# Where the activation operands begin in SBUF, relative to the weights, in a two-network fp32 kernel

## The chip, the cores and the metric

The kernel runs on one core of one Trainium2 chip, as one program. The time is device microseconds for one execution, from three timed runs; beside them stands one further execution that was profiled, and all rows come from that one. Busy times, waits and spacings are read from that profile.

## What is computed

Two small transformers run one behind the other on a sequence of 256 positions of width 1024, all in float32. The first has two layers (differential attention, then neighbourhood attention, each followed by a SwiGLU block of width 2816 and a gated side input); the second has a mixer of a convolution and pooling, then an attention mixer, each followed by a convolutional gated block of width 2816. Cut to what matters here:

```
for i in range(2):                                   # first network
    h = h + (diff_attention, neighborhood_attention)[i](rmsnorm(h, norm_mix[i]))
    hn = rmsnorm(h, norm_ffn[i])
    h = h + (silu(hn @ w_gate[i]) * (hn @ w_up[i])) @ w_down[i]
    h = h + sigmoid(rmsnorm(h, norm_ple[i]) @ ple_w_gate[i]) * (p[i] @ ple_w_proj[i])
x = rmsnorm(h, norm_final)
for layer in range(2):                               # second network
    h = h + (even_mixer, odd_mixer)[layer](rmsnorm(h, mix_norm_g_2[layer]))
    u, g = split(rmsnorm(h, ffn_norm_g_2[layer]) @ w_in_2[layer])
    h = h + (silu(causal_dwconv(u) + conv_b) * g) @ w_out_2[layer]
return rmsnorm(h, final_norm_g_2)
```

Nearly all arithmetic is in the products with weight matrices of 1024 rows or columns.

## The kernel before

Every product with weights is made three times, on the high and low parts of both operands. `Weights.split` (lines 74 to 98) takes a staged float32 chunk of 128 x 1024, writes the rounded part `w_hi` on ScalarE (line 88) and the remainder `w_lo` on VectorE (line 89). Activations are split in the same way into `u_hi` and `u_lo` (`split_act`, lines 225 to 228, written at lines 260 and 262, or at the ends of the attention and mixer stages), and the middle of each feed-forward block into the two halves of a tile `m` (line 735, written at lines 727 and 728). `mm3` then issues three matmuls of 256 columns with 128 x 128 weights, all through line 199: `u_hi,w_hi`, `u_lo,w_hi` and `u_hi,w_lo`. In the rows a matmul is named `out<-moving,stationary`: `ps_g<-u_hi,w_hi` streams `u_hi` past weights `w_hi`. In the value products of the attention stages the roles are exchanged (`ps_v<-w_hi,u_hi`).

A feed-forward block (`ffn`, lines 730 to 748) has 22 steps. Each makes a pair of outputs from `u` (48 matmuls into `ps_g`) and computes a middle `m`; every second step two middles are multiplied with the down matrix into four accumulators (`acc`, 24 matmuls for each middle). So TensorE's work there goes in pieces of 96 matmuls with `u` and 48 with `m`. The middles take their slots in turn from the tags `qh` and `kh`, of two slots each, which in the attention stages hold the high parts of the queries and keys.

No table sets an order here: a tile framework gives out slots from pools, in the order in which pools and tags are first used, and puts a wait where a slot is used again. Together the pools take some 223 KB of each partition, so that room is short. The weight slots are 4,096 bytes each and all begin at 224 bytes past a multiple of 256. A tile `gap` of 64 bytes (lines 114 to 116) stands behind them, so that every slot of the pools `acts` and `work` begins at 32 past a multiple of 256: 64 bytes further than the weights, modulo 256. This remainder is called the distance below. Since all steps inside a tile are multiples of 512 bytes, the distance holds for every matmul of `u` and `m` with weights.

Of the kernel before, what the change touches and what calls it, by code (L numbers as in the profile page):

```python
# [10 lines left out]
F32 = mybir.dt.float32  # L11
F32R = mybir.dt.float32r
# [6 lines left out]
S = 256  # L19
KT = D // 128  # L20
# [86 lines left out]
def network(ctx: ExitStack, tc: tile.TileContext, x_t, p_t, cols, b_v, na_bias, t5_bias, w_mats, out):  # L107
    nc = tc.nc
# [1 line left out]
    const = ctx.enter_context(tc.tile_pool(name="const", bufs=1))  # L110
    stage = ctx.enter_context(tc.tile_pool(name="stage", bufs=N_STAGE))
    split = ctx.enter_context(tc.tile_pool(name="split", bufs=N_HI))

    shift = ctx.enter_context(tc.tile_pool(name="shift", bufs=1))
    gap = shift.tile([128, 16], F32, name="gap")
    nc.gpsimd.memset(gap, 0.0)
    acts = ctx.enter_context(tc.tile_pool(name="acts", bufs=2))
    work = ctx.enter_context(tc.tile_pool(name="work", bufs=2))
    small = ctx.enter_context(tc.tile_pool(name="small", bufs=2))
    psum = ctx.enter_context(tc.tile_pool(name="psum", bufs=1, space=PSUM))  # L120
# [45 lines left out]
    h = const.tile([128, KT, S], F32, name="h")  # L166
# [55 lines left out]
            due.remove(d)  # L222
            d[2]()

    def split_act(tag="u"):
        hi = acts.tile([128, KT, S], F32R, tag=tag + "h", name="u_hi")
        lo = acts.tile([128, KT, S], F32R, tag=tag + "l", name="u_lo")
        return hi, lo

# [188 lines left out]
    def qkv_group(n, g, kind, bv, steps):  # L420
        q = work.tile([128, 2, S], F32, tag="q", bufs=1, name="q")
        k = work.tile([128, 2, S], F32, tag="k", bufs=1, name="k")

        def parts(x, tag):
            hi = work.tile([128, 2, S], F32R, tag=tag + "h", name=tag + "_hi")
            lo = work.tile([128, 2, S], F32R, tag=tag + "l", name=tag + "_lo")
            nc.scalar.activation(hi, x, AF.Copy)
            nc.vector.tensor_sub(lo, x, hi.bitcast(F32))
            return x, hi, lo

        v = work.tile([128, 2, S], F32, tag="v", name="v")
        u = n.u
        ps = pair(u)
        if kind == "na":
            t = work.tile([128, 2, S], F32, tag="qb", bufs=1, name="qb")
            nc.vector.tensor_mul(t, ps, bc2(n.R))
            for i in range(2):
                nc.scalar.activation(q[:, i, :], t[:, i, :], AF.Identity, bias=b_q8[:, 2 * g + i:2 * g + i + 1],
                                     scale=0.125)
        else:  # L440
            nc.vector.scalar_tensor_tensor(q, ps, 0.125, bc2(n.R), op0=OP.mult, op1=OP.mult)
        q = parts(q, "q")
        ps = pair(u)
        if kind == "na":
            t = work.tile([128, 2, S], F32, tag="qb", bufs=1, name="kb")
            nc.vector.tensor_mul(t, ps, bc2(n.R))
            for i in range(2):
                nc.scalar.activation(k[:, i, :], t[:, i, :], AF.Identity, bias=col("b_k", 2 * g + i), scale=1.0)
        else:
            nc.vector.tensor_mul(k, ps, bc2(n.R))  # L450
        k = parts(k, "k")
        steps(q, k, v)
        if kind == "od" and g == 0:
            z = small.tile([128, 2, 8], F32, tag="zf", bufs=1, name="zf")
            pz = [psum.tile([128, 264], F32, tag=f"acc{2 + t}", name="pz") for t in range(2)]
            kk = 0
            for n_k in (3, 3, 2):
                hi, lo = W.take(n_k * 264)
                for i in range(n_k):
                    for t in range(2):  # L460
                        for a, b in ((0, hi), (1, hi), (0, lo)):
                            mm(pz[t], u[a][:, kk, t * 128:(t + 1) * 128], b[:, i * 264:(i + 1) * 264],
                               kk == 0 and (a, b) == (0, hi), kk == 7 and b is lo)
                    kk += 1
                    if kk % 2 == 0:
                        tick()
            for t in range(2):
                nc.scalar.activation(v[:, t, :], pz[t][:, :256], AF.Copy, scale=n.rstd[:, t:t + 1])
                nc.vector.scalar_tensor_tensor(z[:, t, :], pz[t][:, 256:264], n.rstd[:, t:t + 1],
                                               ct[:, COL["b_f"]:COL["b_f"] + 8], op0=OP.mult, op1=OP.add)  # L470
            fox_prepare(z, extra)
            return
        pv = psum.tile([128, 2, S], F32, tag="acc3", name="ps_v")
        for half in range(2):
            hi, lo = W.take(1024)
            for i in range(4):
                kk = 4 * half + i
                for t in range(2):
                    for c, (a, b) in enumerate(((0, hi), (1, hi), (0, lo))):
                        mm(pv[:, t, :], u[a][:, kk, t * 128:(t + 1) * 128], b[:, i * 256:(i + 1) * 256],  # L480
                           kk == 0 and t == 0 and c == 0, kk == 7 and c == 2, skip_group_check=True)
                if i % 2 == 1:
                    tick()
        for t in range(2):
            if kind == "na":
                nc.vector.scalar_tensor_tensor(v[:, t, :], pv[:, t, :], n.rstd[:, t:t + 1], bv,
                                               op0=OP.mult, op1=OP.add)
            else:
                nc.scalar.activation(v[:, t, :], pv[:, t, :], AF.Copy, scale=n.rstd[:, t:t + 1])
# [14 lines left out]
    def small_constants():  # L504

        nc.vector.scalar_tensor_tensor(dist, dist, -1.0, dist, op0=OP.mult, op1=OP.max)
        for hd in range(8):
            nc.vector.tensor_scalar(da_tiles[hd // 4][:, hd % 4], dist, -2.0 ** (-8.0 * (hd + 1) / 8), None, op0=OP.mult)
        nc.vector.tensor_scalar(tri, off[:, :128], 0.0, None, op0=OP.is_ge)
        for g, w in enumerate(POOL_WINDOWS):  # L510
            nc.vector.tensor_scalar(rcnt[:, g, :], rcnt[:, g, :], float(w), None, op0=OP.min)
        nc.vector.reciprocal(rcnt, rcnt)
        nc.vector.tensor_scalar(causal, off, 128.0, NEG, op0=OP.is_gt, op1=OP.mult)
        l = COL["lam"]
        pr = work.tile([128, 2, 64], F32, tag="dump", bufs=1, name="pr")
        for i in range(2):
            nc.vector.tensor_mul(pr[:, i, :], ct[:, l + 128 * i:l + 128 * i + 64], ct[:, l + 128 * i + 64:l + 128 * i + 128])
        nc.vector.tensor_reduce(lam[:, 0:2], pr, AX.X, OP.add)
        nc.scalar.activation(lam[:, 0:2], lam[:, 0:2], AF.Exp)
        lam_init = 0.8 - 0.6 * math.exp(-0.3 * 0)  # L520
        nc.vector.scalar_tensor_tensor(lam[:, 2:3], lam[:, 1:2], -lam_init, lam[:, 0:1],
                                       op0=OP.add, op1=OP.subtract)
        nc.vector.tensor_scalar(sg, col("subln", 0), 1.0 - lam_init, None, op0=OP.mult)
        nc.vector.tensor_scalar(b_q8, ct[:, COL["b_q"]:COL["b_q"] + 8], 0.125, None, op0=OP.mult)
        nc.vector.tensor_mul(g_fm, ct[:, COL["norm_final"]:COL["norm_final"] + 8], ct[:, COL["mix2"]:COL["mix2"] + 8])


    def da_steps(g, q, k, v, bias, o, emitted):
        for p in range(2):
# [23 lines left out]
            def values(p=p, box=box):  # L553
# [4 lines left out]
                        mm(po[:, qt * 128:(qt + 1) * 128], at[:, kk * 256 + qt * 128:kk * 256 + (qt + 1) * 128],  # L558
                           v[:, kk, p * 128:(p + 1) * 128], kk == 0, kk == 1)
                st = small.tile([128, 8], F32, tag="st", bufs=4, name="st2")  # L560
                dump = work.tile([128, 128], F32, tag="dump", bufs=1, name="dump")
                for qt in range(2):
                    nc.scalar.activation(dump, po[:, qt * 128:(qt + 1) * 128], AF.Square, accum_out=st[:, qt:qt + 1])
                nc.vector.tensor_scalar(st[:, 2:4], st[:, 0:2], 1.0 / 128, 1e-5, op0=OP.mult, op1=OP.add)
# [165 lines left out]
    def ffn(n, middle, gain_next, finish=None):  # L730
        acc = Acc(FT)
        mids = {}
        for j in range(FT):
            ps = pair(n.u)
            m = work.tile([128, 2, S], F32R, tag=("qh", "kh")[j % 2], name="m")
            mids[j] = (m[:, 0, :], m[:, 1, :])
            middle(j, ps, n.R, mids[j])
            if j >= 2 and j % 2 == 0 and j < FT - 2:
                acc.step(mids.pop(j - 2), j - 2)
                acc.step(mids.pop(j - 1), j - 1)  # L740
        for j in range(FT - 4, FT - N_LAST):
            acc.step(mids.pop(j), j)
        if finish is None:
            nn, done = next_norm(gain_next)
        else:
            nn, done = finish()
        acc.last([mids.pop(j) for j in range(FT - N_LAST, FT)], FT - N_LAST, done)
        return nn
# [97 lines left out]
    def pool_out(ps, i0):  # L846
        for i in range(2):
            g = i0 + i
# [12 lines left out]
            nc.vector.tensor_mul(av[:, :16], cur[:, 16:32], rcnt[:, g, :])  # L861
            nc.vector.tensor_scalar(av[:, 16:], cur[:, 32:], 1.0 / w, None, op0=OP.mult)
            nc.vector.tensor_sub(av, av, uu[:, 16:])
            m = work.tile([128, 2, S], F32R, tag=("qh", "kh")[g % 2], name="pool_m")
            ph, pl = m[:, 0, :], m[:, 1, :]
            nc.scalar.activation(ph, av, AF.Copy)
            nc.vector.tensor_sub(pl, av, ph.bitcast(F32))
# [89 lines left out]
    rstd_a(n)  # L957
    for i in range(2):
        for t in range(2):
            o = work.tile([128, 512], F32, tag=("qh", "kh")[t], name="o")  # L960
            if t:
                nc.vector.tensor_scalar(o, po[i][t], n.rstd[:, t:t + 1], None, op0=OP.mult)
            else:
# [138 lines left out]
```

## Time and profile before

| | |
|---|---|
| three timed runs | 1276.21, 1270.15, 1274.69 us; median 1274.69 us |
| profiled execution | 1266.52 us, of which 1264.8 us from the first to the last instruction |
| granted TensorE clock, mean | 0.997 of full speed |
| TensorE matmul, weight load | busy 1242.2 us, 1211.8 us |
| VectorE, ScalarE, GpSimd | busy 932.7 us, 697.5 us, 31.6 us |
| read from HBM | 219.74 MB, 175 GB/s over the span |

A matmul's recorded duration (about 280 ns) overlaps those of its neighbours, which start 113 to 118 ns apart, so durations do not add up. What a matmul costs in a stream is the spacing between starts, which is read from the chain of waits (so many matmuls in so many microseconds) or from a window (its length divided by the matmuls in it, where TensorE never idles).

### The profile page before, as it was taken

Reading aid. Unit: us, or ns where it says so; the run is one execution under the profiler, and the core shown is the slowest. Engines: PE = TensorE matmul, PEld = TensorE weight load, DVE = VectorE, ACT = ScalarE, POOL = GpSimd, SP = SyncE. Lnnn points to the kernel's source line nnn. Section 1 sums busy time; section 2 is a strip of 40 time slices with the busy share of each in tenths; the row PEclk is TensorE's granted clock in tenths of the full one; section 3 lists DMA queues with packets and bytes.
Section 4 is the critical chain, followed back from the end, with each engine's and each line's share of the span. In section 5 each row is a group of like instructions: output and inputs, shape, how many; then the busy total and the mean of one; then the engine's idle time right before and its main releaser. Section 6 shows DMA issues by size and latency. Waiting matters only on the chain.

```text
span 1264.8 us, 25714 instructions
## 1 busy us (share of the span) xinstructions
PE 1242.2 (98%) x10448; PEld 1211.8 (96%) x10448; DVE 932.7 (74%) x1708; ACT 697.5 (55%) x1178; POOL 31.6 (2%) x55
## 2 busy tenths in 40 slices
PE   6999999999999999999999999999999999999997
PEld 6999999999988999999999999999999899999997
DVE  7876866667876677666678888777787766877774
ACT  6776644445666654444456456455566565554543
POOL 1011000000010000000000000000000000000000
PEclk9999999999999999999999999999999999999998
DMA  8465566654656436565545475555545343655530
GB/s 291 156 198 182 172 192 201 199 182 147 223 165 177 166 122 205 187 199 186 176 146 192 141 239 190 192 185 192 192 152 186 115 133 131 204 185 189 191 120 34
DMA packets 62936, 222.46 MB, mean 176 GB/s; under 512 B 7265, under 2 KB 7777, under 8 KB 62689
## 3 DMA queue, kind: packets, MB, share of 16 engines
q1 hardware_dynamic: 60768, 214.52, 51.4%
q0 software_dynamic: 1616, 5.77, 2.0%
q8 instruction: 82, 1.34, 0.4%
q10 hardware_dynamic: 432, 0.53, 0.1%
q14 instruction: 38, 0.30, 0.1%
HBM read 219.74 MB, written 1.05 MB: 175 GB/s over the span
## 4 chain that ended last, share of the span: by engine, by line
PE 86%; DVE 5%; issue 3%; ACT 3%; DMA 1%; POOL 1%; POOLq 0%; SPq 0%; DVEq 0%; ACTq 0%
PE ps_g L199 49%; PE acc L199 24%; PE ps_v L199 5%; PE ps_S L199 3%; DVE w_lo L89 2%; PE ps_V L199 2%; PE ps_t L385 1%; ACT w_hi L88 1%; ACT u_hi L260 1%; DMA stage<-w_da_qkv 1%; POOL rstd L285 1%; DVE ssq L253 1%; ACT sq L245 0%; PE pz L199 0%; DVE h L363 0%
## 5 line engine op out<-in xcount | busy, mean ns | idle before, releaser
L88 ACT ACTIVATE w_hi<-stage 128x1024 fp32r<-128x1024 f32 (+2 forms) x413 | 428.9, 1041 | 420.6 <-PE ps_g L199 164.7
L89 DVE TENSOR_TENSOR w_lo<-stage,w_hi 128x1024 fp32r<-128x1024 f32 (+2 forms) x413 | 495.6, 1202 | 204.3 <-ACT w_hi L88 201.6
L199 PE MATMUL ps_g<-u_hi,w_hi 128*128 128x256 f32 x2048 | 575.6, 282 | 8.5 <-ACT w_hi L88 7.0
L199 PE MATMUL ps_g<-u_lo,w_hi 128*128 128x256 f32 x2048 | 571.5, 280 | 0.4 <-DVE u_lo L262 0.4
L199 PE MATMUL ps_g<-u_hi,w_lo 128*128 128x256 f32 x2048 | 570.6, 279 | 0.8 <-DVE w_lo L89 0.8
L199 PEld LDWEIGHTS ps_g<-u_hi,w_hi 128*128 128x128 f32 x2048 | 384.8, 188 | 13.0 <-ACT w_hi L88 7.0
L199 PEld LDWEIGHTS ps_g<-u_hi,w_lo 128*128 128x128 f32 x2048 | 385.4, 188 | 1.3 <-DVE w_lo L89 1.0
L199 PEld LDWEIGHTS ps_g<-u_lo,w_hi 128*128 128x128 f32 x2048 | 385.1, 188 | 1.3 <-DVE u_lo L262 0.6
L199 PE MATMUL acc<-m,w_hi 128*128 128x256 f32 x1408 | 248.5, 279 | 0.2 <-DVE m L728 0.2
L199 PEld LDWEIGHTS acc<-m,w_hi 128*128 128x128 f32 x1408 | 214.4, 188 | 1.0 <-DVE m L728 0.5
L199 PE MATMUL acc<-m,w_lo 128*128 128x256 f32 x704 | 195.6, 278 | 0.0
L199 PEld LDWEIGHTS acc<-m,w_lo 128*128 128x128 f32 x704 | 132.2, 188 | 0.0
L199 PE MATMUL acc<-u_hi,w_hi 128*128 128x256 f32 x256 | 72.7, 287 | 0.0
L199 PE MATMUL acc<-u_lo,w_hi 128*128 128x256 f32 x256 | 71.3, 280 | 0.3 <-DVE u_lo L577 0.3
L199 PE MATMUL acc<-u_hi,w_lo 128*128 128x256 f32 x256 | 71.1, 279 | 0.0
L415 ACT ACTIVATE sc<-sc,st 128x256 f32<-128x256 f32 (+1 forms) x96 | 46.1, 483 | 19.2 <-DVE st L413 19.2
L199 PE MATMUL ps_v<-w_hi,u_hi 128*128 128x256 f32 x176 | 51.1, 291 | 0.0
L199 PE MATMUL ps_v<-w_lo,u_hi 128*128 128x256 f32 x176 | 49.4, 280 | 0.0
L199 PE MATMUL ps_v<-w_hi,u_lo 128*128 128x256 f32 x176 | 49.3, 280 | 0.0
L199 PEld LDWEIGHTS acc<-u_hi,w_hi 128*128 128x128 f32 x256 | 47.8, 188 | 1.5 <-issue 0.6
L199 PEld LDWEIGHTS acc<-u_lo,w_hi 128*128 128x128 f32 x256 | 48.0, 188 | 0.5 <-DVE u_lo L577 0.5
L199 PEld LDWEIGHTS acc<-u_hi,w_lo 128*128 128x128 f32 x256 | 48.0, 188 | 0.0
(190 smaller groups left out, 1218.3 us busy)
## 6 DMA issues: line engine op xcount, KB each, us to landing
stage<-w_gu SPq DMA_DIRECT2D x88, 512.0 KB, 3.8
stage<-w_in SPq DMA_DIRECT2D x88, 512.0 KB, 3.3
stage<-w_down SPq DMA_DIRECT2D x44, 512.0 KB, 3.8
stage<-w_out SPq DMA_DIRECT2D x44, 512.0 KB, 3.3
stage<-w_na_qkv SPq DMA_DIRECT2D x24, 512.0 KB, 3.9
stage<-w_da_qkv SPq DMA_DIRECT2D x23, 512.0 KB, 4.5
stage<-w_od_in SPq DMA_DIRECT2D x22, 512.0 KB, 3.3
stage<-w_gate SPq DMA_DIRECT2D x16, 512.0 KB, 3.3
```

Source lines behind the costliest of these rows:

```text
L88: self.nc.scalar.activation(hi[:, s], t[:, s], AF.Copy)
L89: self.nc.vector.tensor_sub(lo[:, s], t[:, s], hi[:, s].bitcast(F32))
L199: nc.tensor.matmul(o, a, b, start=start, stop=stop, **kw)
L253: nc.vector.tensor_add(ssq, ssq, sq)
L260: nc.scalar.activation(n.u[0][:, 2 * b + i, :], src[:, i, :], AF.Copy, scale=gain(2 * b + i))
L285: nc.gpsimd.tensor_tensor(n.rstd, st[:, 2:4], mhalf, op=OP.pow)
L385: nc.tensor.transpose(ps[:, o:o + 128], a[:, qt, kk * 128:(kk + 1) * 128], ident)
L415: nc.scalar.activation(sc[:, i, :widths[i]], sc[:, i, :widths[i]], AF.Exp, bias=st[:, 2 + i:3 + i], accum_out=st[:, 4 + i:5 + i])
```

## The change

The tile `gap` and its memset go. `acts` has one slot for each of four tags instead of two for each of two, in the same alternation; each slot is 256 bytes longer and the operand begins 32 or 224 bytes into it. The tags `qh` and `kh` get slots that are 64 bytes longer, and the operand begins 32 (`qh`) or 16 bytes (`kh`) into them. Since all slots before them are multiples of 256 long again, the distances become: `u` 224 in the first, third, ... slot that is taken and 32 in the second, fourth, ...; middles 32 and 96 (`qh`), 144 and 208 (`kh`), in the sequence 32, 144, 96, 208 over four steps. To make room, `pr` and `dump` share the tag `fb`. All else in `work` now lies at distance 0, save the low parts of the queries, at 128; before, all of it lay at 64.

```diff
-    shift = ctx.enter_context(tc.tile_pool(name="shift", bufs=1))
-    gap = shift.tile([128, 16], F32, name="gap")
-    nc.gpsimd.memset(gap, 0.0)
-    acts = ctx.enter_context(tc.tile_pool(name="acts", bufs=2))
+    acts = ctx.enter_context(tc.tile_pool(name="acts", bufs=1))
...
-    def split_act(tag="u"):
-        hi = acts.tile([128, KT, S], F32R, tag=tag + "h", name="u_hi")
-        lo = acts.tile([128, KT, S], F32R, tag=tag + "l", name="u_lo")
-        return hi, lo
+    slot = [0]
+
+    def split_act():
+
+        i = slot[0] = slot[0] ^ 1
+        first = (8, 56)[i]
+        parts = []
+        for p, name in (("h", "u_hi"), ("l", "u_lo")):
+            t = acts.tile([128, 64 + KT * S], F32R, tag=f"u{p}{i}", name=name)
+            parts.append(t[:, first:first + KT * S].rearrange("p (k s) -> p k s", k=KT))
+        return tuple(parts)
+
+    def half_tile(tag, name):
+
+        first = {"qh": 8, "kh": 4}[tag]
+        t = work.tile([128, 16 + 2 * S], F32R, tag=tag, name=name)
+        return t[:, first:first + 2 * S].rearrange("p (a b) -> p a b", a=2)
...
-            hi = work.tile([128, 2, S], F32R, tag=tag + "h", name=tag + "_hi")
+            hi = half_tile(tag + "h", tag + "_hi")
...
-        pr = work.tile([128, 2, 64], F32, tag="dump", bufs=1, name="pr")
+        pr = work.tile([128, 2, 64], F32, tag="fb", bufs=2, name="pr")
...
-                dump = work.tile([128, 128], F32, tag="dump", bufs=1, name="dump")
+                dump = work.tile([128, 128], F32, tag="fb", bufs=2, name="dump")
...
-            m = work.tile([128, 2, S], F32R, tag=("qh", "kh")[j % 2], name="m")
+            m = half_tile(("qh", "kh")[j % 2], "m")
...
-            m = work.tile([128, 2, S], F32R, tag=("qh", "kh")[g % 2], name="pool_m")
+            m = half_tile(("qh", "kh")[g % 2], "pool_m")
...
-            o = work.tile([128, 512], F32, tag=("qh", "kh")[t], name="o")
+            o = work.tile([128, 528], F32, tag=("qh", "kh")[t], name="o")[:, :512]
```

No instruction changes its place on any engine. GpSimd has one fewer, at its start; before:

```order
L1088 UNCONDITIONAL_BRANCH [waits barrier_Pool_Activation_PE_DVE_SP_gather]
L116 MEMSET gap 128x16
L176 ISA
L176 IOTA off 128x256
```

and after:

```order
L1097 UNCONDITIONAL_BRANCH [waits barrier_Pool_Activation_PE_DVE_SP_gather]
L172 ISA
L172 IOTA off 128x256
```

The iotas stand one place earlier. On ScalarE, four of the squares into `dump` in the first attention stage name one wait fewer; one of them before:

```order
L388 ACTIVATE at<-ps_t 128x512 [waits PE_49]
L563 ACTIVATE dump,st_714<-ps_V 128x128 [waits PE_49,Activation_49]
L563 ACTIVATE dump,st_714<-ps_V 128x128 [waits Activation_49]
```

and after:

```order
L397 ACTIVATE at<-ps_t 128x512 [waits PE_49]
L572 ACTIVATE dump,st_709<-ps_V 128x128 [waits PE_49]
L572 ACTIVATE dump,st_709<-ps_V 128x128 [waits Activation_49]
```

The wait that went was one of ScalarE on its own earlier square.

## Rows read from the trace of the kernel before

**Rows 1.** The page: busy time by engine, then the chain by line.

```profile
PE 1242.2 (98%) x10448; PEld 1211.8 (96%) x10448; DVE 932.7 (74%) x1708; ACT 697.5 (55%) x1178; POOL 31.6 (2%) x55
...
PE ps_g L199 49%; PE acc L199 24%; PE ps_v L199 5%; PE ps_S L199 3%; DVE w_lo L89 2%; PE ps_V L199 2%; PE ps_t L385 1%; ACT w_hi L88 1%; ACT u_hi L260 1%; DMA stage<-w_da_qkv 1%; POOL rstd L285 1%; DVE ssq L253 1%; ACT sq L245 0%; PE pz L199 0%; DVE h L363 0%
```

**Rows 2.** What TensorE waited for: total us, times, longest.

```profile
PE ps_g L199 <- ACT w_hi L88: 7.0, 1, 7.0
PE ps_r L301 <- POOL rstd L285: 3.4, 4, 2.5
```

**Rows 3.** Chain, first feed-forward block: start us, us, what.

```profile
152.76 10.88 PE ps_g L199 x96
163.64 5.44 PE acc L199 x48
```

**Rows 4.** Chain, second feed-forward block.

```profile
490.88 11.31 PE ps_g L199 x96
502.18 5.65 PE acc L199 x48
```

**Rows 5.** Chain, third feed-forward block, where pieces of both lengths stand.

```profile
780.98 10.88 PE ps_g L199 x96
791.86 5.61 PE acc L199 x48
797.47 11.31 PE ps_g L199 x96
...
825.74 5.55 PE acc L199 x48
831.29 10.88 PE ps_g L199 x96
```

**Rows 6.** TensorE by window: bounds, length, busy (matmuls), clock, DMA share, GB/s.

```profile
139.00:313.00 174.00, 174.00 (x1538) 1.00 0.59 190
320.00:344.00 24.00, 24.00 (x206) 1.00 0.71 238
476.00:658.00 182.00, 182.00 (x1546) 1.00 0.55 182
664.00:689.00 25.00, 25.00 (x222) 1.00 0.62 208
702.00:760.00 58.00, 57.82 (x489) 1.00 0.57 186
...
1085.00:1120.00 35.00, 35.00 (x300) 1.00 0.57 191
1121.00:1140.00 19.00, 19.00 (x168) 1.00 0.59 194
1141.00:1246.00 105.00, 105.00 (x894) 1.00 0.44 146
```

**Rows 7.** Groups by line: shapes, count, busy us, mean ns, idle before.

```profile
L199 PE MATMUL ps_g<-u_lo,w_hi 128*128 128x256 f32 x2048 | 571.5, 280 | 0.4 <-DVE u_lo L262 0.4
L199 PE MATMUL acc<-m,w_hi 128*128 128x256 f32 x1408 | 248.5, 279 | 0.2 <-DVE m L728 0.2
L199 PE MATMUL acc<-m,w_lo 128*128 128x256 f32 x704 | 195.6, 278 | 0.0
L199 PE MATMUL acc<-u_hi,w_lo 128*128 128x256 f32 x256 | 71.1, 279 | 0.0
L199 PE MATMUL ps_v<-w_hi,u_lo 128*128 128x256 f32 x176 | 49.3, 280 | 0.0
...
L199 PE MATMUL ps_p<-p_part,w_hi 128*128 128x256 f32 x64 | 11.5, 278 | 0.0
```

**Rows 8.** Chain in the second attention stage.

```profile
376.63 0.44 PE ps_t L385 x4
377.07 1.37 PE ps_g L199 x12
378.44 1.41 PE ps_v L199 x12
```

**Rows 9.** By line, the memset of gap: min/median/max ns, first and last start.

```profile
L116 POOL MEMSET gap<- x1: 112/112/112, 0.7 to 0.7; 128x16 f32 x1
```

**Rows 10.** The same view of the tile dump.

```profile
L563 ACT ACTIVATE dump<-ps_V x16: 257/277/280, 46.4 to 119.5; 128x128 f32<-128x128 f32 x16
```

## The prediction

> **What bounds the kernel now.** The page comes first: TensorE is busy for 98% of the span, and the chain that ends last lies on it, with 78% in three kinds of products with weights, `ps_g`, `acc` and `ps_v` [rows 1]. Then what TensorE waits for: the longest entry is 7.0 us, once, at the start; the next totals 3.4 us [rows 2]. No feeding engine is late in the long stages, so what a change is worth there is read from the spacing of matmuls and from nothing else.
>
> The chain gives that spacing, and the reader is to see that there are two. In the first feed-forward block 96 matmuls take 10.88 us and 48 take 5.44 us, 113.3 ns each [rows 3]. In the second, the same 96 and 48 take 11.31 and 5.65 us, 117.8 ns each [rows 4]. Shapes, order and distance (64 bytes) are the same. In the third, whole pieces of either length follow one another and the rhythm changes within an `acc` piece (5.61 and 5.55 us lie between) [rows 5]. So TensorE has a fast and a slow rhythm, 0.43 us / 96 = 4.5 ns apart, and keeps either for a long time: the windows give 174.00 us / 1538 = 113.1 ns for the whole first block and 182.00 / 1546 = 117.7 ns for the whole second [rows 6]. The granted clock is 1.00 in both, so it is not the clock; and no wait marks the difference.
>
> **How much hangs on the rhythm.** The 256-column products with weights are three kinds of 2048 for `ps_g`, 1408 + 704 for `acc` from `m`, three of 256 for `acc` from `u`, three of 176 for `ps_v`: 6144 + 2112 + 768 + 528 = 9552 [rows 7]. What the slow rhythm cost in this execution, as a window's length less its matmuls at 113.3 ns [rows 6]: second block 182.0 - 175.2 = 6.8 us; 702 to 760, 57.8 - 55.4 = 2.4; 320 to 344, 0.7; fourth block 35.0 - 34.0 = 1.0 and 105.0 - 101.3 = 3.7. In the third block four pieces of 96 are slow, of which rows 5 show one, for 4 x 0.43 = 1.7, and its eight `acc` pieces are between 0.11 and 0.22 over 5.44, together 1.3. That is 17.6 us over some 6,820 matmuls. The other 2,730 lie mostly in the three attention stages, broken up by short work; there 12 matmuls take 1.41 us (117.5 ns) in one piece and 1.37 us (114.2 ns) in the piece before it [rows 8]. I take three in four as slow: 2730 x 0.75 x 4.5 ns = 9.2 us. In all the slow rhythm cost about 27 us. **Bounds:** everything fast would be 1266.5 - 27 = 1239.5 us. For everything slow, the matmuls now at 113.3 ns pay 4.5 ns more: 1538 + 222 + 168 in their windows, some 800 in the third block and 2730 x 0.25 = 680 in attention, 3,400 in all, or 15 us: 1281.5 us.
>
> The profiled execution took 1266.5 us, 8.2 us under the median of 1274.69; at 4.5 ns that is 1,800 matmuls more in the slow rhythm, well inside these bounds. The three timed runs differ by 6 us with the same program and the same addresses, so which rhythm a stage falls into is partly chance. The mean of the four executions, (1276.2 + 1270.2 + 1274.7 + 1266.5) / 4 = 1271.9 us, is the best reading of the kernel before.
>
> **The change part by part.** Nothing is moved, and no step is added. *The memset* of the gap, 112 ns on GpSimd at 0.7 us [rows 9], goes; TensorE's first wait ends on ScalarE's split of weights at 7 us [rows 2], which needs transfers and not GpSimd, so this is worth nothing; if that cover were gone it would be 0.1 us. *The tag shared by `pr`, `dump` and `fb`*: the 16 squares take 277 ns each, between 46 and 120 us [rows 10]; four lose a wait of ScalarE on itself, and `fb` itself serves the last attention stage alone. Zero; all four at a full square each would be 1.1 us. *The longer slots* change no instruction's size.
>
> *The distances* are the change. `u` goes from 64 to 224 or 32 (6,900 matmuls with `acc` from `u`), middles from 64 to 32, 144, 96, 208 (2,112), and `ps_v` from 192, seen the other way round, to 32 or 224. What a distance of 32 or 144 costs a matmul no row shows, so it is bounded by the nearest. (a) `ps_v` lies at 192 and shows 117.5 ns a matmul in one piece right behind `ps_g` at 114.2 [rows 8], and its recorded duration is 280 ns as that of `ps_g` [rows 7]: another distance, the same two rhythms. That speaks for no price at all. (b) Below: the transposes stream `ident` at distance 224 to the tile they transpose, 4 in 0.44 us, 110 ns [rows 8]. They are another kind of operation, so this is a far bound: 9552 x 3.3 ns = 32 us under the all-fast time, 1208 us. (c) Above: a third rhythm one equal step of 4.5 ns over the slow one would cost the middles 2112 x 4.5 = 9.5 us, 1291 us, and all matmuls 43 us, 1324.5 us. I take (a), the only row with the same operation at two distances. *The rest of `work`* goes to distance 0: 96 matmuls from `p_part` [rows 7] and some 240 of the scores' high and low parts; at one step each, 336 x 4.5 ns = 1.5 us either way, taken as 0.
>
> The Trainium skill speaks against the change here: in "TensorE: Matmul & The Clock Gate", Part 2, it says that TensorE reads streamed operand and weights through two independent SBUF ports, so that loading the next weights takes nothing from the running matmul. By that rule no distance can matter and the time stays; that `ps_v` at 192 keeps the known rhythms agrees, that there are two rhythms at all the page does not tell.
>
> **The rivals.** *A, forecast: the distance does not enter.* The two rhythms stay, drawn by chance; the time is that of before, 1271.9 us, with the spread of four executions, 1266 to 1277. For it: both rhythms hold for 1,500 matmuls at one and the same distance, and `ps_v`. A change of distance between `u` and `m` may be a new draw, now every 24 to 96 matmuls; were slow then the outcome nearly always, the time would still be under the all-slow 1281.5 us. Chance 0.43.
>
> *B: the distance decides which rhythm lasts, and the new ones favour 113.3 ns.* TensorE is busy with matmuls for 98% and with weight loads for 96% of the span [rows 1], so both operands are read at the same time; where both begin may set whether the slow rhythm can hold. For it: in rows 5 the rhythm changes at `acc`, where the operand changes; if a new distance breaks the slow rhythm and leaves the fast one, most of 27 us goes. Against it: in before a piece of `u` and one of `m` have the same distance, and still the rhythm changes there. All fast gives 1239.5 us, half of the 27 us gone 1253. Chance 0.36.
>
> *C, slower: a new distance has a price of its own, a third rhythm above 117.8 ns.* If the next weights and the streamed operand get in each other's way at some distances, 64 and 192 may be among the harmless ones, and of the five new distances some may not be. For it: the slow rhythm itself shows that a matmul can lose 4.5 ns with nothing waiting. Against it: no row of before shows a spacing over 117.8 ns in a long stage. One step of 4.5 ns on the middles alone gives 1271.9 + 9.5 = 1281.4 us, on the middles with all else slow 1291 us, on `u` alone 1271.9 + 6912 x 4.5 ns = 1303 us. It decides from some 2,050 matmuls that pay one step, nearly all the middles. Chance 0.17.
>
> *D: the change does more than A to C allow*, a rhythm under 113 ns, towards 1208 us: 0.04.
>
> **How the numbers follow.** The time is A's, rounded: 1272 us. About 0.5% is what a measurement can tell from no change: 1268.3 to 1281.1 around the median. A gives 0.39 within, 0.01 faster and 0.03 slower (nearly all slow); B 0.33 faster, 0.03 within; C 0.16 slower, 0.01 within; D 0.04 faster. Faster 0.38, same 0.43, slower 0.19. The range leaves out D, the part of B next to all fast and the part of C in which `u` pays: 1242 to 1289 us. A's own range is 1266 to 1280 us.
>
> **What would show it.** In the chain of the changed kernel, pieces of 96 `ps_g`: A is right if both 10.88 and 11.31 us are still there in about the old shares and nothing else; B if 11.31 is rare or gone; C if 96 `ps_g` take more than 11.31 us or 48 `acc` more than 5.65. If `acc` differs from `ps_g`, the distances of the middles differ in price. The forecast fails if the feed-forward blocks' windows give a spacing under 114 ns or over 118 ns throughout.

## The result and the profile after

The changed kernel takes 1282.04 us (median of five, 1281.13 to 1283.1) against 1275.94 us before (median of five, 1270.15 to 1276.27): 1.0067 times the time, 95% interval 1.0038 to 1.0095. It is slower by 0.7%, inside the stated range but not the way that was forecast, which was no change. The executions of before spread over 6 us, those of after over 2.

The page of the changed kernel, busy time by engine and then the chain by line, to be read against [rows 1]:

```profile
PE 1259.0 (98%) x10448; PEld 1229.2 (96%) x10448; DVE 932.8 (73%) x1708; ACT 697.0 (54%) x1178; POOL 31.1 (2%) x54
...
PE ps_g L195 53%; PE acc L195 25%; PE ps_v L195 5%; PE ps_S L195 3%; PE ps_V L195 2%; PE ps_t L394 1%; ACT w_hi L88 1%; ACT u_hi L269 1%; DVE w_lo L89 1%; DMA stage<-w_da_qkv 1%; PE ps_p L195 1%; POOL rstd L294 1%; PE pz L195 0%; DVE h L372 0%; PE ps_ss L195 0%
```

The busy times of VectorE, ScalarE and GpSimd are those of before; the span grew by 15.4 us and TensorE's busy time by 16.8 us. (The medians differ by 6.1 us only: the profiled execution of before, 1266.5 us, was 9 us under its median.) What TensorE waits for did not grow either (total us, times, longest; before in [rows 2]):

```profile
PE ps_g L195 <- ACT w_hi L88: 7.2, 2, 6.8
PE ps_r L310 <- POOL rstd L294: 3.4, 4, 2.5
```

So the matmuls themselves start further apart. The chain of the changed kernel shows it; first, third and fourth feed-forward block, in that order (start us, us, what):

```profile
155.17 11.36 PE ps_g L195 x96
166.53 5.74 PE acc L195 x48
172.27 11.35 PE ps_g L195 x96
183.62 5.66 PE acc L195 x48
```

```profile
791.91 11.36 PE ps_g L195 x96
803.27 5.74 PE acc L195 x48
809.01 11.35 PE ps_g L195 x96
820.36 5.67 PE acc L195 x48
```

```profile
1105.19 11.20 PE ps_g L195 x96
1116.40 5.65 PE acc L195 x48
1122.05 11.20 PE ps_g L195 x96
1133.25 5.74 PE acc L195 x48
```

Three things are new against [rows 3 to 5]. Neither 10.88 nor 11.31 us for 96 `ps_g` is there any more. In the first three blocks, where `u` lies at 224, every piece takes 11.35 or 11.36 us, 118.3 ns a matmul; in the fourth, where it lies at 32, every piece takes 11.20 us, 116.7 ns. And `acc` alternates between about 5.65 and 5.74 us (117.7 and 119.6 ns), which are the pairs of middles at 32 and 144 and at 96 and 208. The length of a piece goes with the distance of its operand, and it is the same from piece to piece. By window, in the views of [rows 6] (bounds, length, busy with matmuls, clock, DMA share, GB/s):

```profile
139.00:313.00 174.00, 174.00 (x1470) 1.00 0.55 188
...
1141.00:1246.00 105.00, 105.00 (x895) 1.00 0.49 171
```

The first block holds 1470 matmuls in 174 us, where before held 1538: 118.4 against 113.1 ns. The last holds 895 against 894.

### The profile page after: what moved, and what is told of

Same layout as the page of the kernel before. It is cut to its first block, busy times and chain, and to the rows that moved or that the text cites. A ratio compares the mean times of both kernels' runs of the same rounds, so it can differ in the third digit from the quotient of the medians.

```text
span 1280.2 us, 25709 instructions
## 1 busy us (share of the span) xinstructions
PE 1259.0 (98%) x10448; PEld 1229.2 (96%) x10448; DVE 932.8 (73%) x1708; ACT 697.0 (54%) x1178; POOL 31.1 (2%) x54
## 4 chain that ended last, share of the span: by engine, by line
PE 91%; issue 3%; ACT 2%; DVE 2%; DMA 1%; POOL 1%; SPq 0%; POOLq 0%; DVEq 0%; ACTq 0%
PE ps_g L195 53%; PE acc L195 25%; PE ps_v L195 5%; PE ps_S L195 3%; PE ps_V L195 2%; PE ps_t L394 1%; ACT w_hi L88 1%; ACT u_hi L269 1%; DVE w_lo L89 1%; DMA stage<-w_da_qkv 1%; PE ps_p L195 1%; POOL rstd L294 1%; PE pz L195 0%; DVE h L372 0%; PE ps_ss L195 0%
## 5 line engine op out<-in xcount | busy, mean ns | idle before, releaser
L195 PE MATMUL acc<-m,w_hi 128*128 128x256 f32 x1408 | 253.5, 282 | 0.0
```

Source lines behind the costliest of these rows:

```text
L195: nc.tensor.matmul(o, a, b, start=start, stop=stop, **kw)
```

## The experiments

Two theories stood against each other. **P**: each distance between the streamed operand and the weights (modulo 256 bytes) has a spacing of its own, and the kernel's time is their sum. **Q**: distances are free, and what costs is the change of distance from one operand to the next.

Spacings below are means over all 256-column matmuls of one operand in one profile, from start to next start, leaving out gaps under 105 and over 130 ns (where other work stands between). Each kernel is compared with executions of before on the same chip; the medians of those are 1275.2 us (e1 to e4), 1277.7 (e5 to e8), 1276.1 (e9, e10) and 1276.0 us (e11, e12). The mean granted clock of TensorE lay between 0.995 and 0.998 in every execution and does not go with the times: e9, the fastest kernel, has 0.995 to 0.996, and e1 and e4, two of the slowest, 0.997 to 0.998.

### One distance for everything

Four kernels are the kernel before with another length of `gap`; the shortest has no gap.

```diff
-    gap = shift.tile([128, 16], F32, name="gap")
+    gap = shift.tile([128, 24], F32, name="gap")
```

> The kernel before with a gap of 96 bytes in place of 64: activations, middles and all else in the work pool lie at the one distance 96. Theory P (each distance has a price of its own): in the changed kernel the matmuls that stream a middle at 96 start 119.8 ns apart on average, against about 117.1 in a median execution of before, so 9552 x 2.7 ns = 26 us more, about 1302 us, and spacings of 121 to 125 ns are seen. Theory Q (a price is paid for the changes of distance between operands, the distance itself is free): one distance throughout gives the two rhythms of before, 113.3 and 117.8 ns, and 1266 to 1282 us.

Measured: 1295.59 us, 1.0165 times before (1.015 to 1.018). The chain in the second feed-forward block, where before took 11.31 and 5.65 us [rows 4]:

```profile
503.91 11.52 PE ps_g L199 x96
515.43 5.76 PE acc L199 x48
521.19 11.52 PE ps_g L199 x96
```

120.0 ns a matmul, all at one distance, so no change between operands is needed.

> The kernel before with a gap of 224 bytes: everything at the one distance 224. Theory P: 118.25 ns as the activations at 224 show in the changed kernel, 1.15 ns over a median execution of before, 9552 x 1.15 = 11 us, about 1287 us, slower than the changed kernel itself. Theory Q: only 113.3 and 117.8 ns, 1266 to 1282 us.

Measured: 1283.27 us, 1.0068 times before (1.0053 to 1.0083): as large a loss as the changed kernel's, with one of its five distances everywhere.

```profile
499.51 11.36 PE ps_g L199 x96
510.88 5.68 PE acc L199 x48
516.55 11.36 PE ps_g L199 x96
```

The 11.36 us of the changed kernel stand there to the hundredth, and now for `acc` too (5.68).

> The kernel before with a gap of 32 bytes: everything at the one distance 32. Theory P: 117.0 ns as the operands at 32 show in the changed kernel, about 1276 us, the cheapest of the five new distances. Theory Q: only 113.3 and 117.8 ns, 1266 to 1282 us. The times do not tell the two apart here; the spacings do: P expects values such as 116 and 120 ns, which before hardly has.

Measured: 1273.16 us, 0.9981 times before (0.9971 to 0.9991); 117.1 ns on average, with 116 and 120 ns among the commonest spacings, which before hardly has. The length of a piece alone would not show this: in the second block 96 `ps_g` take 11.31 us as in [rows 4], but of spacings of 116, 118 and 119 ns, and in the first block the mean is 116.7 ns. So 32 has no single spacing either.

> The kernel before without the gap: everything at distance 0. Theory P: the only operand at 0 in the changed kernel, the side input, shows 119.2 ns, 2.1 ns over a median execution of before, 9552 x 2.1 = 20 us, about 1296 us. Theory Q: only 113.3 and 117.8 ns, 1266 to 1282 us.

Measured: 1295.77 us, 1.0167 times before (1.0152 to 1.0182); 119.9 ns, four in five of all spacings at 120. All four went as P said, to within 7 us; Q is refuted by the times and spacings of the first, second and fourth and by the spacings of the third.

### The parts of the change

The activations alone, with the shared tag; the gap of 64 bytes stays, so offsets of 224 and 160 bytes give distances of 32 and 224:

```diff
-        hi = acts.tile([128, KT, S], F32R, tag=tag + "h", name="u_hi")
+        first = (56, 40)[i]
...
+            t = acts.tile([128, 64 + KT * S], F32R, tag=f"u{p}{i}", name=name)
```

> The activations alone at 224 and 32 as in the changed kernel, with its shared tag; the gap stays, so middles and all else lie at 64 as before. Theory P (each distance has its own price, and prices add up): 4,485 matmuls at 224 pay 118.25 - 117.1 = 1.15 ns, 5 us over before, those at 32 nothing: about 1280.5 us, with `acc` from `m` in the two rhythms of before. Theory Q (what costs is the change of distance between operands): the whole loss is there already, 1282 us, and `acc` from `m` shows other spacings than 113.3 and 117.8 ns.

Measured: 1280.9 us, 1.003 times before (1.0015 to 1.0045). `ps_g` at 224 shows 118.3 ns, `acc` from `m` at 64 is at 117 to 119 or 113 to 114 ns for all but 4% of its matmuls: what stands before a middle at 64 does not bring in other spacings.

The middles alone are the changed kernel with the activations at 64:

```diff
-        first = (8, 56)[i]
+        first = (16, 16)[i]
```

> The changed kernel with the activations at 64, in both slots; middles at 32, 144, 96 and 208, the rest at 0 as there. Theory P: 528 matmuls each at +0, +1.5, +2.7 and +1.9 ns over 117.1, 3.2 us, and 96 of the side input at 0 with +2.9 ns, 0.3 us: about 1278.5 us, `ps_g` in the two rhythms. Theory Q: 1282 us or more, and `ps_g` shows other spacings too.

Measured: 1277.84 us, 1.0008 times before (0.9992 to 1.0024): no loss that can be told from none, against 3.5 us expected, which lies just outside the interval. Middles at 96 and 208 took 119.8 and 118.9 ns as in the changed kernel (119.8 and 119.0), those at 32 took 117.0 (117.0); but those at 144 took 116.0 ns instead of 118.6. In the first two blocks they are in a rhythm of 113 and 114 ns (114.1 and 113.4 ns on average), which they hardly show in the changed kernel; in the last two blocks they take 117.7 and 118.7 ns, though the activations before them lie at 64 there too. So P holds with an addition: some distances allow more than one rhythm. What decides which is not shown; the operand before it may have a part, but it is not enough. By itself the activations' part is the larger, a loss of 0.3% or some 4 us, and the two parts together, 1.0038, agree with the whole, 1.0067, within their intervals.

### Distance or address

```diff
+    lead = ctx.enter_context(tc.tile_pool(name="lead", bufs=1))
+    lead_t = lead.tile([128, 24], F32, name="lead")
+    nc.gpsimd.memset(lead_t, 0.0)
     stage = ctx.enter_context(tc.tile_pool(name="stage", bufs=N_STAGE))
```

> The kernel before with a tile of 96 bytes ahead of the staging buffers, so that staged chunks, weights and all that follows lie 96 bytes further, and the distance stays 64. Theory P (the distance decides): 113.3 and 117.8 ns as before, 1266 to 1278 us. Rival (the address itself decides, of the operands or of the weights): activations would lie at 128 past a multiple of 256, as those of the kernel with everything at distance 96, and take its 119.8 ns and 1295 us.

Measured: 1276.52 us, 0.9996 times before (0.9975 to 1.0016), with the second block's pieces at 11.31 and 5.65 us as before:

```profile
499.29 11.31 PE ps_g L202 x96
510.60 5.65 PE acc L202 x48
```

Staging buffers, weights, activations and all of `work` lie 96 bytes further, and nothing changed: for this shift at least it is the distance that counts and not the address.

### More distances

```diff
-        first = (8, 56)[i]
+        first = (12, 28)[i]
...
-        first = {"qh": 8, "kh": 4}[tag]
+        first = {"qh": 4, "kh": 12}[tag]
```

> The changed kernel with other offsets: activations at 48 and 112, middles at 16, 176, 80 and 240; the rest at 0 as there. It measures six more distances. Theory P: each shows its own mean spacing, in the span of those measured, 116 to 120 ns, the same whichever operand stands before it; the time is their sum, anywhere from 1268 to 1300 us. Theory Q: the spacings resemble those of the changed kernel, 117 to 120 ns, and the time is about 1282 us.

Measured: 1270.1 us, 0.9949 times before (0.9931 to 0.9967). The activations at 112, which are those of three blocks in four, started 114.1 ns apart, less than the 116 to 120 ns expected; those at 48, 118.3 ns. The middles took 118.6 (16), 119.8 (80), 119.0 (176) and 117.3 ns (240). So a distance was found that keeps the 113.3 ns rhythm nearly always: in those three blocks 93% of the spacings are 112 to 115 ns. The same edit with 26 and 30 words for the activations and 0 for both tags gives 104, 120 and the multiples of 64:

> The changed kernel with activations at 104 and 120, middles at 0, 128, 64 and 192. Measures prices either side of 112 in steps of 8 bytes, and the multiples of 64. Theory P: 0 at 120.0 ns as in the kernel with everything at 0; 64 and 192 in 113.3 and 117.8 ns; 128 not measured yet, between 113 and 120. If what matters is where 16-byte pieces fall, 104 and 120 differ from all multiples of 16 and may cost more than any, over 120 ns, 1300 us; if the price runs smoothly in the distance, both lie near the 114.1 ns of 112, and the time is about 1255 us.

Measured: 1301.77 us, 1.0205 times before (1.0181 to 1.0229). At 104 `ps_g` takes 120.1 ns, at 120 it takes 122.5 (`u_hi`) and 119.8 ns (`u_lo`). The chain in the second block shows 120, where the best distance has 10.88 us:

```profile
508.01 11.57 PE ps_g L195 x96
525.31 11.71 PE ps_g L195 x96
```

Eight bytes either side of the best distance lie two of the dearest: the price does not run smoothly. That 104 and 120 are dear because they are not multiples of 16 is unlikely: the value products lay at 136 and 152 in this kernel and took 119.3 and 118.9 ns, less than the 120 ns of 0 and 96. The middles took 119.4 ns at 0, 117.8 at 64, 119.0 at 128 and 115.2 at 192, the last in the two rhythms of 64.

All means together, by distance (streamed operand minus weights, modulo 256; the value products are counted the same way, so that `u` at 224 there is a distance of 32; a span where several operands or profiles differ):

```
bytes   ns mean                        bytes   ns mean
   0    119.4 to 120.0                   128   119.0
  16    118.6                            136   119.3
  32    116.7 to 117.3                   144   115.9 to 120.0, several rhythms
  48    118.3                            152   118.9
  64    116.0 to 117.8, two rhythms      160   118.2
  80    119.8                            176   119.0
  96    119.8 to 120.0                   192   115.2 to 116.5, two rhythms
 104    120.1                            208   117.8 to 119.0
 112    113.8 to 114.3                   224   118.0 to 118.3
 120    119.8 to 122.5                   240   117.3
```

In the value products of e3, where `u` is the stationary operand, the distance of 224 took 118.1 ns, and that of 32 took 117.0 ns in those of e2: it is streamed minus stationary that counts, whichever tile has which role. In the changed kernel the slots of `u_hi` and `u_lo` at 224 are 256 bytes apart modulo 512 and took 118.24 and 118.28 ns, so at this distance the price is the same 256 bytes on. At 120 it is not so simple: `u_hi` and `u_lo`, again 256 bytes apart modulo 512, differ, and `u_hi` itself takes 124.4 ns with `w_hi` and 120.5 with `w_lo`, which lie at the same distance. So the distance modulo 256 does not settle the spacing everywhere.

### A kernel that beats both

All slots of `u` are cut from one long tile, all middles from another, behind a gap of 96 bytes, so that every one can begin at 112 without a slot of odd length:

```diff
-    gap = shift.tile([128, 16], F32, name="gap")
+    gap = shift.tile([128, 24], F32, name="gap")
...
+    u_all = acts.tile([128, 4 * N_U + 64], F32R, tag="u", name="u_hi")
...
+            first = 4 + (2 * p + i) * N_U
+            parts.append(u_all[:, first:first + N_U].rearrange("p (k s) -> p k s", k=KT))
```

> The kernel before with activations and middles in all their slots at 112 (each kind cut from one long tile behind a gap of 96 bytes), the rest at 96. Theory P: 114.1 ns for 9,020 matmuls as the activations at 112 show among the six distances, against 117.4 in a typical execution of before, -30 us; the value products then lie at 144 and pay 528 x 2.5 ns = 1.3 us: about 1247 us, 2.3% under before, and the middles, at 64 before, show the same 114 ns as the activations. Rival R (112 did well only because of the operands around it, as the middles at 144 took 118.6 ns in the changed kernel and 116.0 beside activations at 64): no better than the 1270 us of the six distances.

Measured: 1256.53 us, 0.9853 times before (0.9826 to 0.9881). The second feed-forward block, against [rows 4]:

```profile
492.06 10.88 PE ps_g L199 x96
502.94 5.44 PE acc L199 x48
508.38 10.88 PE ps_g L199 x96
519.26 5.44 PE acc L199 x48
```

113.3 ns, and so in the first block and in every piece of this one. Middles took 113.8 ns, `u` 113.9 to 114.7. It is 9 us short of the 1247 expected: that sum took the gain for all 9,020 matmuls, but in the attention stages 12 matmuls between two pieces of short work still take 1.43 us, no less than before (1.37 and 1.41 in [rows 8]), and the value products, at 144, take 120.0 ns, which is 2 us where 1.3 were put:

```profile
390.96 1.43 PE ps_g L199 x12
393.28 1.60 PE ps_g L199 x12
395.32 1.43 PE ps_g L199 x12
```

The gain is in the unbroken stretches: from their first matmul to their last the four blocks take 752.8 us in e7, which has the distances of before, and 730.7 us here. That is 22 us, 3.5 ns for each of their 6,336 matmuls; 20 were measured for the whole kernel.

> The same long tiles as in the kernel with everything at 112, but activations and middles at 64; the rest at 32. Theory P (112 made the gain, not the long tiles): 113.3 and 117.8 ns again, 1268 to 1280 us, no difference from before. Rival L (the long tiles made it, by other waits or slots): near 1256 us.

Measured: 1276.86 us, 0.9997 times before (0.9981 to 1.0013). The long tiles alone are worth nothing; the distance of 112 is. And the smallest edit to the changed kernel:

```diff
-        first = (8, 56)[i]
+        first = (28, 28)[i]
```

> The changed kernel with one edit: the activations begin 112 bytes into both slots in place of 32 and 224. Theory P: in the feed-forward blocks 3,168 matmuls that were at 224 gain 118.25 - 114.0 = 4.2 ns and 1,056 that were at 32 gain 3.0 ns, 16.5 us; some 900 in the side gates and the even mixer gain 3 us; attention, broken up by short work, gains nothing: 1282 - 19 = about 1263 us. Theory Q (it is the changes between activations and four kinds of middles that cost): they are still there, no gain, about 1280 us.

Measured: 1263.02 us, 0.9894 times before (0.9877 to 0.9911), where P gave 1263. Two numbers in one line turn the changed kernel from 0.7% slower to 1.1% faster. In its second block the activations are at 113.3 to 113.8 ns, and the middles keep their prices of the changed kernel:

```profile
493.87 10.92 PE ps_g L195 x96
504.79 5.65 PE acc L195 x48
510.44 10.88 PE ps_g L195 x96
521.32 5.73 PE acc L195 x48
```

## Why the prediction was wrong

**What held.** The bound was right: TensorE, and of it nothing but the spacing of matmuls. The memset, the shared tag and the longer slots cost nothing that shows: the page has one instruction fewer on GpSimd and the same busy times elsewhere, and e2, which has none of these edits, lost as much as the changed kernel. Of the two bounds, everything slow was put at 1281.5 us, and 30 executions of before stayed under it, at 1269.6 to 1279.7 us; that the changed kernel comes to 1282.0 is luck, since its spacings are others. Everything fast was put at 1239.5 us, which is too low: with 113.3 ns in the long pieces e9 takes 1256.5, in part because the 9 us booked for the attention stages are not there to gain.

**The step that failed** is (a) of the distances. From the value products at 192, which show the two rhythms of 64, it took that a distance has no price. 192 was the one other distance in the trace that it had for the same operation, and it is one of the few that share the rhythms of 64; of the sixteen multiples of 16 that were measured in the end, only 64, 112, 144 and 192 hold the 113.3 ns rhythm for long, and 144 in two blocks of one kernel alone (e6). One harmless value was read as a rule. At 224, where 4,512 matmuls went, 118.3 ns replaced a mixture of 113.3 and 117.8; by the prediction's own sign for C its pieces of 96 took more than 11.31 us, and the first block's window, at 118.4 ns, is past the 118 it named. The far bound (b), 110 ns for transposes at 224, says nothing of these products either: at 224 they took 118.3.

**The terms, with what they measured.** No profile of before near its median is there; e7, with the same distances, is the nearest (1277.97 us in its profiled execution, 117.5 ns for `u` and 117.6 for `m`). Against it `u` at 224 costs 4,382 x 0.8 ns = 3.5 us, `u` at 32 saves 2,326 x 0.4 = 0.9 us, the middles cost some 525 x (-0.6 + 2.2 + 0.9 + 1.4) = 2.0 us, the value products 0.6 us. That is 5.2 us. The two profiled executions are 4.0 us apart (1281.97 against 1277.97) and the medians of before and after 6.1 us, so the sum has the size but not the last microsecond. The middles had been the suspects of rival C, at one step of 4.5 ns; their dearest distance, 96, costs half a step, and the larger part is the activations', whose price is small but paid far more often.

**The rivals.** C had the mechanism, a price of the distance itself, and the sign; its sizes were wrong, and so was its expectation of pieces over 11.31 us by a whole step: 11.36 us is 0.05 over. B was wrong for these five distances and right in kind: at 112, which the change does not use, the 113.3 ns rhythm lasts and 20 us go. The new draw at each change of operand, put into A, is not what happens: with everything at 224 the same spacing stands without any change.

**The reading of before** leaned on the profiled execution, 1266.5 us, as one of four. In 30 executions on one chip the median was 1277.7 us and three were under 1273; the profiled one, faster than all of them, was rare luck, most of it in the first block. The mean of 1271.9 us was 4 us under the median of 1275.9, and nearly half of that is the profiled execution: without it the mean is 1273.7 us. It hid that before already runs mostly at 117.8 ns, and so that little was left to lose and much to gain.

**What stays open.** Why a distance has its price is not shown. Nor is why 112 differs so from 104 and 120, why `u_hi` at 120 takes longer with `w_hi` than with `w_lo`, or what puts the middles at 144 into 113.4 ns in one block and 118.7 in another. That the reads of the two operands get in each other's way is a guess that fits; no run here separates it from others.

## What to carry to other kernels

Where TensorE streams without a pause, look at the spacing between starts over the whole trace before asking which engine waits: two spacings for the same instruction are a sign of something that no wait shows. Where the streamed operand begins relative to the weights, modulo 256 bytes, moved this kernel between 1256 and 1302 us with the same matmuls in the same order, so it is worth a sweep, and several distances can be measured in one run if each operand gets its own. All of this is one shape, 256 streamed columns with 128 x 128 weights loaded for each matmul in float32; others were not tried. One other value that does no harm in a trace bounds nothing: take it as one sample of a function that need not be smooth.

## What the runs showed that was not expected

- The price of a distance is not smooth: 120.1 ns at 104 bytes, 114.0 at 112, 119.8 to 122.5 at 120.
- The spread between executions of one program goes with it as well: where the distance allows two rhythms, as 64, 30 executions lie between 1269.6 and 1279.7 us; where the mean is steady, as at 96, four lie between 1295.1 and 1296.5. That the rhythms make this spread is argued from the two profiles at 64 (before and e7), not shown run by run.
- The Trainium skill ("TensorE: Matmul & The Clock Gate", Part 2) says that loading the next weights takes no SBUF read bandwidth from the running matmul. By that alone the distance should not matter; these runs do not agree: with addresses alone moved, a matmul beside a weight load took from 113.3 to 120.0 ns [rows 3, and e4].
